# Rotating eight queries and both keys of a mixer at once, and normalising a unit's probabilities in one operation

## The chip, the cores and the metric

The kernel runs on one core of a Trainium2 chip. The metric is the time of one execution on the device in microseconds (us), lower is better; the kernel before has a median of 800.55 us over three runs (799.91 to 801.0). Five engines work side by side, each with its own queue in order: TensorE (PE in the profile; its weight loads are PEld), VectorE (DVE), ScalarE (ACT), GpSimd (POOL) and SyncE (SP), which here issues the DMAs. They wait for one another by semaphores.

## The reference

Two layers on 256 positions of width 1024, all in fp32. Each layer normalises its input (RMSNorm) and makes one projection `h @ w_in`, whose columns are divided among:

- mixer A: 8 queries, 2 keys and 2 values of 64 columns a head; attention in a window of 128 with a sink per head; queries and keys rotated by their position;
- mixer B: 8 queries; a compressed, a selected and a window branch, each with 2 keys and 2 values; the queries are used raw for the compressed branch and rotated for the two others, whose keys are rotated too. Three sigmoid gates a head weigh the branches;
- two merge gates of 1024 columns each.

The rotation is `concatenate([x1*cos - x2*sin, x2*cos + x1*sin])` on the two halves of a head. The probabilities of a head are `exp(s - m)` divided by their sum (for mixer A the sum and the sink's exponential). The outputs of the mixers are projected, gated, added, projected again and added to the input; then follows a gated feed-forward part with a short causal convolution (2816 inner columns), again with a norm on either side. With 256 positions the selected branch chooses all four blocks, so here it is plain causal attention, as the window branch is.

## The kernel before, in words

**Precision.** A factor of a matmul is split into a high and a low half (`copy` on ScalarE, L114, makes the high one; `sub` on VectorE, L117, the rest), and each product is three matmuls: high by high, high by low, low by high (`mm3`, L365). Weights come by DMA into `st`, four chunks deep, and are split into `wh` and `wl`.

**Tiling.** The 256 positions are two blocks t of 128. The input projection is cut into nine column tiles (IN_TILES); tile i takes four chunks of weights, and for each chunk and block six matmuls add into that block's bank. At its last chunk the tile's `fin` function reads the bank: `fin_a` (tile 0, eight queries of A), `fin_b` (tile 1), `fin_d` (tile 2: selected key and value, window key and value, 128 columns each, of mixer B), `fin_gate`, `fin_c` (tile 4). Banks of PSUM are taken by tag, two of each: "mm", "S", "T", "O". Tiles 2 and 3 both take "mm", so a block of tile 3 starts when the last reader of the like block of tile 2 is done.

**Rotation.** `rope` (L457) makes four VectorE instructions for h heads: `src * rs * cos` (L461), two halves of `src * rs * sin` (L463), and the sum (L465). `q_rot` (L477) does this for four queries, splits the result into a stacked tile `stk` of high and low halves and leaves `stack_T` for later, which transposes it with four matmuls (L472) and copies it into the query buffer. `k_rot` does the like for two keys of one branch. `v_split` writes the high half of two values with ScalarE and the low half with one VectorE instruction (L508) into VT, a zero-padded buffer; there is one VT for each of the three branches.

**Units.** A `Unit` is one block, one group of four heads and one or two branches. `scores` computes the scores in banks "S" (L588), a minimum per head on VectorE (L597) and the exponential on ScalarE (L600). `probs_T` makes one scale per head (L613 to L619), multiplies each head's probabilities by it with one VectorE instruction per head and branch (L622), transposes them (L628) and splits them. `values` multiplies by VT (L660 to L662). Each layer has four units of A (two of 4 heads x 128 columns, two of 4 x 256) and six of B: two with both branches (8 x 128) and four with one (4 x 256).

**Order.** Written work is put on a clock of parts: `part` advances it by one, `later(n, fn)` and `at(tick, fn)` put functions on later ticks, and PLAN and DL hold the ticks. The first tile of the first layer runs in the order as written on TensorE, VectorE and ScalarE (`manual_schedule`); everywhere else a planner orders each engine's instructions at build time, with modelled costs, by the order in which they were written among those that it holds ready. So a changed duration may change the order of other instructions. On the chip each engine keeps its order.

In the compressed branch of mixer B, `cmp_gelu` has ScalarE's tanh (L747) on the result of a chain of small GpSimd instructions (L730 to L741), and L748 on VectorE reads it.

## Time and profile before

| | |
|---|---|
| median of three runs | 800.55 us |
| the profiled execution | 800.75 us, of which the span from first to last instruction is 798.9 |
| mean granted TensorE clock | 0.991 |
| TensorE busy | 767.3 us (96%), 4745 matmuls |
| VectorE busy | 620.1 us (78%), 1280 instructions |
| ScalarE busy | 497.7 us (62%) |
| GpSimd busy | 44.2 us (6%) |

Busy time is the time in which at least one instruction of the engine runs; instructions of one engine overlap a little, so the next one may start before the one ahead of it ends. An instruction waits in its engine's queue until what it needs is there, and all behind it wait too. [...]

### The profile page before, as it was taken

The page shows a single profiled execution, that of the slowest core. Times are in us where ns is not written, and L with a number is a line of the kernel's source. Part 1 is how long each engine was busy: PE and PEld are TensorE (multiplying, and loading weights), DVE is VectorE, ACT ScalarE, POOL GpSimd, SP SyncE. Part 2 cuts the span into 40 slices and gives each one's busy share as a digit, 9 for nine tenths or more (in the row PEclk, how much of TensorE's full clock was granted, in tenths as well). Part 3 has the DMA queues.
Part 4 walks back from the last instruction along what each step waited for, and adds up shares of the span by engine and source line. Part 5 has one row for each costly group of instructions (what it writes and reads, how often), then busy time and mean ns, then how long its engine had stood idle before and what let it go on. Part 6 is the DMA issues. An engine that isn't in the chain of part 4 may idle for free.

```text
span 798.9 us, 13019 instructions
## 1 busy us (share of the span) xinstructions
PE 767.3 (96%) x4745; PEld 681.5 (85%) x4745; DVE 620.1 (78%) x1280; ACT 497.7 (62%) x952; POOL 44.2 (6%) x97
## 2 busy tenths in 40 slices
PE   7989989999899999999989999899998999999996
PEld 6778878888689999999968888888877999999995
DVE  5888888867768777777789999786867877767775
ACT  4678787755656555565555879667555655556552
POOL 2200022100200000000010000120001000000000
PEclk9998999999999999999999999999999999999998
DMA  7632156446556565665535232543545655656631
GB/s 266 226 100 89 61 155 202 133 162 182 191 177 186 185 185 186 207 216 185 182 106 179 90 119 78 196 162 132 187 156 170 199 185 185 185 185 210 213 106 53
DMA packets 42203, 131.26 MB, mean 164 GB/s; under 512 B 5359, under 2 KB 5915, under 8 KB 42139
## 3 DMA queue, kind: packets, MB, share of 16 engines
q1 hardware_dynamic: 41995, 130.18, 50.3%
q8 instruction: 37, 0.61, 0.3%
q10 hardware_dynamic: 144, 0.26, 0.1%
q14 instruction: 27, 0.22, 0.1%
HBM read 129.37 MB, written 1.05 MB: 163 GB/s over the span
## 4 chain that ended last, share of the span: by engine, by line
PE 81%; DVE 7%; ACT 6%; POOL 2%; issue 2%; DMA 1%; SPq 0%; DVEq 0%; POOLq 0%; ACTq 0%
PE mm L366 6%; PE mm L368 6%; PE mm L367 6%; PE S L367 5%; PE S L368 5%; PE S L366 5%; PE T L994 5%; PE T L993 5%; PE mm L994 5%; PE mm L993 5%; PE T L992 5%; PE mm L992 5%; PE O L366 3%; PE O L367 3%; PE O L368 3%; DVE wl L117 2%
## 5 line engine op out<-in xcount | busy, mean ns | idle before, releaser
L117 DVE TENSOR_TENSOR wl<-st,wh 128x1024 fp32r<-128x1024 f32 (+2 forms) x226 | 267.9, 1187 | 103.7 <-ACT wh L114 102.6
L114 ACT ACTIVATE wh<-st 128x1024 fp32r<-128x1024 f32 (+2 forms) x226 | 232.2, 1030 | 176.9 <-PE T L993 38.8
L366 PE MATMUL mm<-wh,x 128*128 128x512 f32 (+2 forms) x256 | 98.2, 384 | 3.4 <-DVE VT L508 2.4
L367 PE MATMUL mm<-wl,x 128*128 128x512 f32 (+2 forms) x256 | 95.8, 374 | 0.0
L368 PE MATMUL mm<-wh,x 128*128 128x512 f32 (+2 forms) x256 | 95.4, 373 | 0.1
L993 PE MATMUL mm<-q,wh 128*128 128x256 f32 x320 | 90.7, 283 | 0.0
L994 PE MATMUL T<-q,wl 128*128 128x256 f32 x320 | 90.6, 283 | 0.0
L993 PE MATMUL T<-q,wh 128*128 128x256 f32 x320 | 90.5, 283 | 0.0
L994 PE MATMUL mm<-q,wl 128*128 128x256 f32 x320 | 90.5, 283 | 0.0
L992 PE MATMUL T<-q,wh 128*128 128x256 f32 x320 | 90.5, 283 | 0.0
L992 PE MATMUL mm<-q,wh 128*128 128x256 f32 x320 | 90.5, 283 | 0.0
L992 PEld LDWEIGHTS mm<-q,wh 128*128 128x128 f32 x320 | 61.3, 192 | 0.9
L993 PEld LDWEIGHTS mm<-q,wh 128*128 128x128 f32 x320 | 61.3, 192 | 0.8
L992 PEld LDWEIGHTS T<-q,wh 128*128 128x128 f32 x320 | 61.3, 192 | 0.8
L993 PEld LDWEIGHTS T<-q,wh 128*128 128x128 f32 x320 | 61.3, 192 | 0.7
L994 PEld LDWEIGHTS mm<-q,wl 128*128 128x128 f32 x320 | 61.3, 192 | 0.1
L994 PEld LDWEIGHTS T<-q,wl 128*128 128x128 f32 x320 | 61.3, 192 | 0.0
L366 PEld LDWEIGHTS mm<-wh,x 128*128 128x128 f32 x256 | 49.5, 193 | 9.4 <-DVE VT L508 2.8
L368 PEld LDWEIGHTS mm<-wh,x 128*128 128x128 f32 x256 | 49.1, 192 | 6.6 <-DVE x L117 0.5
L367 PEld LDWEIGHTS mm<-wl,x 128*128 128x128 f32 x256 | 49.3, 193 | 5.2 <-DVE wl L117 0.4
L600 ACT ACTIVATE k<-k,mn 128x128 f32<-128x128 f32 (+1 forms) x96 | 42.6, 448 | 6.6 <-DVE mn L597 6.5
L114 ACT ACTIVATE k<-k 128x256 fp32r<-128x256 f32 x72 | 29.8, 414 | 10.8 <-DVE k L1005 5.8
(293 smaller groups left out, 1663.9 us busy)
## 6 DMA issues: line engine op xcount, KB each, us to landing
st<-in_ffn_w_up_dram SPq DMA_DIRECT2D x88, 512.0 KB, 4.2
st<-in_w_in_dram SPq DMA_DIRECT2D x48, 512.0 KB, 3.7
st<-in_ffn_w_down_dram SPq DMA_DIRECT2D x44, 512.0 KB, 3.7
st<-in_w_out_dram SPq DMA_DIRECT2D x16, 512.0 KB, 4.0
st<-in_w_in_dram SPq DMA_DIRECT2D x16, 384.0 KB, 3.2
st<-in_cmp_w_dram SPq DMA_DIRECT2D x16, 256.0 KB, 2.7
st<-in_w_branch_a_dram SPq DMA_DIRECT2D x8, 512.0 KB, 3.5
st<-in_w_branch_b_dram SPq DMA_DIRECT2D x8, 512.0 KB, 3.5
```

Of the source, the lines that this page charges most:

```text
L114: act.activation(dst, src, AF.Copy, scale=scale)
L117: dve.tensor_tensor(dst, a, b, ALU.subtract)
L366: pe.matmul(o, xh, wh, start=first, stop=False, skip_group_check=True)
L367: pe.matmul(o, xh, wl, start=False, stop=False, skip_group_check=True)
L368: pe.matmul(o, xl, wh, start=False, stop=last, skip_group_check=True)
L600: last_exp[0] = act.activation(self.pt[:, hh, s, :], sm[:, :nk], AF.Exp, bias=self.mn[:, i:i + 1], scale=-1.0, accum_out=self.dn[:, i:i + 1])
L992: pe.matmul(o, wh[:, k, :], hh[:, k, c0:c1], start=(k == 0), stop=False, skip_group_check=True)
L993: pe.matmul(o, wh[:, k, :], hl[:, k, c0:c1], start=False, stop=False, skip_group_check=True)
L994: pe.matmul(o, wl[:, k, :], hh[:, k, c0:c1], start=False, stop=(k == 7), skip_group_check=True)
```

## The change

`fin_a` rotates all eight queries of a block with one `rope` of eight heads, and then splits and stacks them in two parts of four. `fin_d` rotates the selected and the window keys with one `rope` of four heads. For that the columns of tile 2 are put in another order in the bank: the matmuls read the weights' pieces of 128 columns as key, key, value, value, where they lie as key, value, key, value. The four values of a block go with one ScalarE and one VectorE instruction into one buffer of 33 x 64 columns (VT33) in place of two; `values` takes its blocks from there by an offset. `probs_T` multiplies all probabilities of a unit by their scales, broadcast along the columns, in one instruction in place of four or eight. Mixer A's keys and values, and the queries of mixer B, go through the changed functions with the same instructions as before.

```diff
--- before.py
+++ after.py
@@ -316,7 +316,7 @@
         o = R_CB + l * 44 + jj
         return vec[:, o:o + 1]
 
-    VT = [cp.tile([P, 17 * 64], F32R, name=f"VT{i}") for i in range(3)]
+    VT = [cp.tile([P, n * 64], F32R, name=f"VT{n}") for n in (17, 33)]
     for v in VT:
         pool.memset(r32(v), 0.0)
 
@@ -436,7 +436,12 @@
                 tk = slice(t * P, (t + 1) * P)
                 for k in range(2):
                     kk = 2 * c + k
-                    mm3(bk[t][:, :w], xh[:, kk, tk], xl[:, kk, tk], ch[0][:, k, :], ch[1][:, k, :], kk == 0, kk == 7)
+                    o, wh, wl = bk[t][:, :w], ch[0][:, k, :], ch[1][:, k, :]
+                    if i == 2:
+
+                        o = o.rearrange("p (y x d) -> p y x d", x=2, y=2)
+                        wh, wl = [v.rearrange("p (x y d) -> p y x d", x=2, y=2) for v in (wh, wl)]
+                    mm3(o, xh[:, kk, tk], xl[:, kk, tk], wh, wl, kk == 0, kk == 7)
                 if c == 3:
                     fin(t, bk[t])
                 if tmajor and t == 1 and c < 2:
@@ -474,13 +479,16 @@
                 done.add(key)
             return fn
 
-        def q_rot(qT, t, h0, src, key, delay):
-            d = rope(src, t, True, 4)
-            stk = k2(F32R)
-            sv = stk.rearrange("p (h a d) -> p h a d", h=4, a=2)
-            copy(sv[:, :, 0, :], d)
-            sub(sv[:, :, 1, :], d, r32(sv[:, :, 0, :]))
-            later(delay, stack_T(stk, qT[:, h0:h0 + 4, t * P:(t + 1) * P], key, 0))
+        def q_rot(qT, t, h0, src, key, delays):
+            d = rope(src, t, True, 4 * len(delays))
+            for i, delay in enumerate(delays):
+                stk = k2(F32R)
+                sv = stk.rearrange("p (h a d) -> p h a d", h=4, a=2)
+                di = d[:, 4 * i:4 * i + 4, :]
+                copy(sv[:, :, 0, :], di)
+                sub(sv[:, :, 1, :], di, r32(sv[:, :, 0, :]))
+                h = h0 + 4 * i
+                later(delay, stack_T(stk, qT[:, h:h + 4, t * P:(t + 1) * P], (key[0], t, h // 4), 0))
 
         def q_raw(qT, t, h0, src, key, delay):
             if rq[t] is None:
@@ -492,27 +500,29 @@
             dve.scalar_tensor_tensor(sv[:, :, 1, :], src, rq[t], r32(sv[:, :, 0, :]), ALU.mult, ALU.subtract)
             later(delay, stack_T(stk, qT[:, h0:h0 + 4, t * P:(t + 1) * P], key, 0))
 
-        def k_rot(kT, t, src, key, delay):
-            rk = rope(src, t, False, 2)
-            stk = k2(F32R)
-            sv = stk.rearrange("p (g s a d) -> p g s a d", g=2, s=2, a=2)
-            kb = rk[:, :, None, :].to_broadcast([P, 2, 2, 64])
-            copy(sv[:, :, 0], kb)
-            sub(sv[:, :, 1], kb, r32(sv[:, :, 0]))
-            later(delay, stack_T(stk, kT[:, :, :, t * P:(t + 1) * P], key, 1))
-
-        def v_split(V, t, src, key):
+        def k_rot(t, src, dsts):
+            d = rope(src, t, False, 2 * len(dsts))
+            for i, (kT, key, delay) in enumerate(dsts):
+                stk = k2(F32R)
+                sv = stk.rearrange("p (g s a d) -> p g s a d", g=2, s=2, a=2)
+                kb = d[:, 2 * i:2 * i + 2, None, :].to_broadcast([P, 2, 2, 64])
+                copy(sv[:, :, 0], kb)
+                sub(sv[:, :, 1], kb, r32(sv[:, :, 0]))
+                later(delay, stack_T(stk, kT[:, :, :, t * P:(t + 1) * P], key, 1))
+
+        def v_split(V, n, t, src, keys):
             vb = V.rearrange("p (b d) -> p b d", d=64)
-            vh, vl = vb[:, t * 8 + 1:t * 8 + 6:4, :], vb[:, t * 8 + 3:t * 8 + 8:4, :]
+            o = t * 4 * n + 1
+            vh, vl = vb[:, o:o + 4 * n - 3:4, :], vb[:, o + 2:o + 4 * n - 1:4, :]
             copy(vh, src, scale=rs[t])
             dve.scalar_tensor_tensor(vl, src, rs[t], r32(vh), ALU.mult, ALU.subtract)
-            done.add(key)
+            done.update(keys)
 
         qA, qB, qR = big8("q8", 3), big8("q8", 3), big8("q8", 3)
         kA = ap_.tile([P, 2, 2, T], F32R, tag="kA", name=nm("kA"))
         kB = ap_.tile([P, 2, 2, 2, T], F32R, tag="kB", name=nm("kB"))
         kS, kW = kB[:, 0], kB[:, 1]
-        vA, vS, vW = VT
+        vA, vB = VT
         OB = [[None, None], [None, None]]
         OT = [None, None]
         GE = [None, None]
@@ -522,17 +532,16 @@
 
 
         def fin_a(t, b):
-            q_rot(qA, t, 0, heads(b, 0, 4), ("qA", t, 0), DL["qa0"])
-            q_rot(qA, t, 4, heads(b, 256, 4), ("qA", t, 1), DL["qa1"])
+            q_rot(qA, t, 0, heads(b, 0, 8), ("qA", t, 0), (DL["qa0"], DL["qa1"]))
 
         def fin_b(t, b):
-            k_rot(kA, t, heads(b, 0, 2), ("kA", t), DL["ka"])
-            v_split(vA, t, heads(b, 128, 2), ("vA", t))
-            q_rot(qB, t, 0, heads(b, 256, 4), ("qB", t, 0), DL["qb0"])
+            k_rot(t, heads(b, 0, 2), [(kA, ("kA", t), DL["ka"])])
+            v_split(vA, 2, t, heads(b, 128, 2), [("vA", t)])
+            q_rot(qB, t, 0, heads(b, 256, 4), ("qB", t, 0), (DL["qb0"],))
             q_raw(qR, t, 0, heads(b, 256, 4), ("qR", t, 0), DL["qr0"])
 
         def fin_c(t, b):
-            q_rot(qB, t, 4, heads(b, 0, 4), ("qB", t, 1), DL["qb1"])
+            q_rot(qB, t, 4, heads(b, 0, 4), ("qB", t, 1), (DL["qb1"],))
             q_raw(qR, t, 4, heads(b, 0, 4), ("qR", t, 1), DL["qr1"])
             for kd in range(2):
                 kvd[t][kd] = k2()
@@ -544,10 +553,8 @@
                 later(DL["cb1"], lambda: cmp_blocks(1))
 
         def fin_d(t, b):
-            k_rot(kS, t, heads(b, 0, 2), ("kS", t), DL["ks"])
-            v_split(vS, t, heads(b, 128, 2), ("vS", t))
-            k_rot(kW, t, heads(b, 256, 2), ("kW", t), DL["kw"])
-            v_split(vW, t, heads(b, 384, 2), ("vW", t))
+            k_rot(t, heads(b, 0, 4), [(kS, ("kS", t), DL["ks"]), (kW, ("kW", t), DL["kw"])])
+            v_split(vB, 4, t, heads(b, 256, 4), [("vS", t), ("vW", t)])
 
         def fin_gate(i):
             c0, w = IN_TILES[i]
@@ -617,9 +624,8 @@
                     e = self.co[:, 0:4]
                     dve.tensor_tensor(e, e, self.dn, ALU.add)
                 dve.reciprocal(e, e)
-                for i in range(n):
-                    p = self.pt[:, i // ns, i % ns, :]
-                    dve.tensor_scalar(p, p, e[:, i:i + 1], None, ALU.mult)
+                p = self.pt.rearrange("p h s c -> p (h s) c")
+                dve.tensor_tensor(p, p, e[:, :, None].to_broadcast([P, n, self.nk]), ALU.mult)
                 self.ph = []
                 for s in range(ns):
                     for kb in range(t + 1):
@@ -643,8 +649,8 @@
                         c = slice(par * 256, par * 256 + 256)
                         v = []
                         for part_ in range(2):
-                            blk = 1 + 2 * ((kb * 2 + g) * 2 + part_) - par
-                            v.append(V[:, blk * 64:blk * 64 + P])
+                            blk = 1 + 2 * ((kb * V[2] + V[1] * 2 + g) * 2 + part_) - par
+                            v.append(V[0][:, blk * 64:blk * 64 + P])
                         mm3_(ov, v, ph[:, c], pl[:, c], first)
                         first = False
                 done.add(("O", self.br, t, g, self.sets[0][3]))
@@ -830,7 +836,7 @@
 
 
         B = lambda k: base + k
-        sA, sS, sW = (kA, vA, "kA", 0), (kS, vS, "kS", 1), (kW, vW, "kW", 2)
+        sA, sS, sW = (kA, (vA, 0, 2), "kA", 0), (kS, (vB, 0, 4), "kS", 1), (kW, (vB, 1, 4), "kW", 2)
         for (t, g), tick in zip(((0, 0), (0, 1), (1, 0), (1, 1)), PLAN["A"]):
             e = Unit(t, g, 0, qA, "qA", [sA], m_band).plan(B(tick))
             if t == 1:
```

## Rows read from the trace of the kernel before

**Rows 1.** The page: busy us (share) by engine; chain of waits by engine.

```profile
PE 767.3 (96%) x4745; PEld 681.5 (85%) x4745; DVE 620.1 (78%) x1280; ACT 497.7 (62%) x952; POOL 44.2 (6%) x97
...
PE 81%; DVE 7%; ACT 6%; POOL 2%; issue 2%; DMA 1%; SPq 0%; DVEq 0%; POOLq 0%; ACTq 0%
```

**Rows 2.** TensorE's waits: who <- for whom: us in total, times, longest us.

```profile
PE T L628 <- DVE k L622: 3.9, 3, 2.0
...
PE mm L366 <- DVE VT L508: 2.4, 2, 1.8
```

**Rows 3.** Timeline, TensorE, 53 to 58.4: start, us, what, [idle before <-releaser].

```profile
53.71 0.96 PE L588 MATMUL S<-kA,q 128*128 128x128 f32 x7
55.36 0.28 PE L472 MATMUL T<-ident_r,k 128*128 128x128 f32 x1 [0.69 <-ACT k L114]
...
58.36 0.60 PE L366 MATMUL mm<-wh,x 128*128 128x280 f32 x1 [1.79 <-DVE VT L508]
```

**Rows 4.** Windows: stretch, us, busy (x) of PE, PEld, DVE, ACT, POOL, clock, DMA.

```profile
57.40:64.20 6.80, 5.84 (x25) 5.83 (x26) 5.01 (x23) 3.87 (x14) 0.00 (x0) 0.50 0.00 0
65.50:75.00 9.50, 7.89 (x60) 7.41 (x60) 9.27 (x34) 9.50 (x32) 0.00 (x0) 1.00 0.31 104
455.00:465.00 10.00, 10.00 (x81) 9.62 (x80) 9.91 (x33) 10.00 (x31) 0.00 (x0) 1.00 0.30 93
507.95:511.30 3.35, 3.35 (x16) 3.28 (x16) 2.60 (x12) 2.35 (x7) 0.00 (x0) 0.50 0.02 6
```

**Rows 5.** Timeline of VectorE, then of ScalarE, 53 to 58 us.

```profile
53.14 0.34 DVE L461 SCALAR_TENSOR_TENSOR k<-mm,rstd,tab 128x128 f32<-128x128 f32 x1
...
57.96 0.35 DVE L508 SCALAR_TENSOR_TENSOR VT<-mm,rstd,VT 128x128 fp32r<-128x128 f32 x1
...
54.16 0.36 ACT L114 ACTIVATE VT<-mm,rstd 128x128 fp32r<-128x128 f32 x1
...
56.92 0.36 ACT L114 ACTIVATE VT<-mm,rstd 128x128 fp32r<-128x128 f32 x1
```

**Rows 6.** Timeline of VectorE, 67 to 75 us.

```profile
67.60 0.87 DVE L622 TENSOR_SCALAR k<-k,co 128x128 f32<-128x128 f32 x4
...
71.28 1.22 DVE L117 TENSOR_TENSOR wl<-st,wh 128x1024 fp32r<-128x1024 f32 x1
72.41 0.68 DVE L117 TENSOR_TENSOR k<-T,k 128x512 fp32r<-128x512 f32 x1
73.01 1.13 DVE L622 TENSOR_SCALAR k<-k,co 128x256 f32<-128x256 f32 x4
```

**Rows 7.** Groups by line and shape: count | busy us, mean ns | idle.

```profile
L461 DVE SCALAR_TENSOR_TENSOR k<-mm,rstd,tab 128x256 f32<-128x256 f32 x12 | 5.7, 479 | 1.8 <-POOL tab L348 1.8
```

**Rows 8.** Timeline of VectorE in both layers, around 94, 444 and 481 us.

```profile
94.53 0.20 DVE L619 RECIPROCAL co<-co 128x8 f32<-128x8 f32 x1
...
444.38 0.34 DVE L461 SCALAR_TENSOR_TENSOR k<-mm,rstd,tab 128x128 f32<-128x128 f32 x1
...
481.60 0.20 DVE L619 RECIPROCAL co<-co 128x8 f32<-128x8 f32 x1
```

**Rows 9.** Timeline of VectorE, then of TensorE, 27 to 29 us.

```profile
27.10 1.22 DVE L117 TENSOR_TENSOR wl<-st,wh 128x1024 fp32r<-128x1024 f32 x1
...
28.37 0.50 PE L367 MATMUL S<-wl,x 128*128 128x512 f32 x1 [1.16 <-DVE wl L117]
```

**Rows 10.** Timeline of VectorE, then of TensorE, 119 to 121 us.

```profile
119.44 0.19 DVE L748 SCALAR_TENSOR_TENSOR z<-z,z 128x32 f32<-128x32 f32 x1 [1.63 <-ACT z L747]
119.55 1.13 DVE L622 TENSOR_SCALAR k<-k,co 128x256 f32<-128x256 f32 x4
...
120.05 0.41 PE L628 MATMUL T<-cst,k 128*128 128x128 f32 x2 [1.74 <-DVE k L622]
```

**Rows 11.** Timeline of TensorE: scores on kB in two pieces, then in one.

```profile
87.40 1.11 PE L588 MATMUL S<-kB,q 128*128 128x256 f32 x8
...
130.15 0.64 PE L588 MATMUL S<-kB,q 128*128 128x256 f32 x4
```

## The prediction

> **What bounds the kernel now.** I read the page's first part, then the waits of TensorE, then its timeline where the waits are long, then VectorE and ScalarE in the same stretch. TensorE is busy 767.3 of 798.9 us [rows 1], so only its 31.6 us of idle time, and what it loses where it is busy at half clock, can be won; VectorE (78%) and ScalarE (62%) matter only where TensorE waits for them, and VectorE is 7% of the chain of waits [rows 1]. The waits say which of its idle time ends on an instruction of this change: 3.9 us in three waits for the normalised probabilities (L622) and 2.4 us in two waits for the low half of the second mixer's values (L508) [rows 2]. Everything else that TensorE waits for is left as it is.
>
> The place that matters most is in layer 0, after the input tile of the second mixer's keys and values. That tile and the next one share two "mm" banks, so the next tile can't start before the last reader of a bank is done, and for block 0 that is L508 for the window values. TensorE finishes its scores at 54.67 (53.71 + 0.96), waits 0.69 us, does a few short instructions and waits 1.79 us more until 58.36 [rows 3]. The granted clock is 0.50 (1.2 of 2.4 GHz) from 57.40 to 64.20, right behind this idle time, and TensorE is busy for 5.84 us of it [rows 4]: at full clock that is half, so 2.9 us are lost on top of the 2.5 us of waits. A second half-clock stretch of 3.35 us stands behind the longest L622 wait in layer 1 [rows 4].
>
> **The bank release in layer 0 (fin_d).** Now: VectorE starts on block 0 at 53.14 and the last read ends at 58.31 (57.96 + 0.35), 5.17 us later [rows 5]. The work itself is small; it is strung out because the second v_split comes last: ScalarE makes the first split's high half at 54.16 and the second's only at 56.92, because instructions for other work were put between. The fused version needs one ScalarE copy of 128x256, which can stand where the first stands now, and one VectorE split behind it. How long: an instruction's own cost is its step to the next start, some 0.09 us less than its duration (the 1024-wide subtraction lasts 1.22 us and the next one starts 1.13 us later [rows 6]). Scalar-tensor-tensor on PSUM lasts 0.34 us for 128 [rows 5] and 0.479 us for 256 elements [rows 7], some 1.07 ns an element; so steps of 0.26 and 0.39 us, 0.19 for 64 and 0.67 for 512. Plain tensor-tensor has steps of 1.13 us for 1024 and 0.60 for 512 elements [rows 6], which by the same line makes 0.33 for 256 and 0.20 for 128.
> - Two key rotations now: 2 x (0.26 + 2 x 0.19 + 0.20) = 1.68 us. One of four heads: 0.39 + 2 x 0.26 + 0.33 = 1.24. Saved 0.44, four times: 1.8 us.
> - Two low halves now 2 x 0.26 = 0.52; one of 256: 0.39. Saved 0.13, four times: 0.5 us. ScalarE saves about as much.
> The new release of block 0's bank is then 53.14 + 1.24 + 0.39 = 54.77, and with an allowance of 0.4 for a hand-over and an instruction of other work in between about 55.2 instead of 58.31. TensorE is free at 54.67 and its 2.5 us of waits shrink to about 0.6. With that little idle time I expect no half-clock stretch. Gross gain: 1.9 + 2.9 = 4.8 us. How much survives is best read from layer 1, which runs the same code without the half clock: from the first key rotation to the reciprocal of the second mixer's first unit it takes 481.60 - 444.38 = 37.22 us, in layer 0 94.53 - 53.14 = 41.39 us [rows 5, 8]. So layer 0 can win 4.2 us before it runs like layer 1. I take 4.0. Bounds: 0 (the new order puts the copy late again) and 5.4 us (all waits and the whole half-clock loss). In layer 1 the release is hidden better; I take 0.3 us for it, between 0 and 1.
>
> **The rotation of eight queries (fin_a).** Now per block 2 x (0.39 + 2 x 0.26 + 0.33) = 2.48 us of VectorE; fused 0.67 + 2 x 0.39 + 0.60 = 2.05. Saved 0.43, four times 1.7 us. But the three long instructions come before the weight split on which TensorE waits 1.16 us at 28.37 [rows 9]: 0.67 + 2 x 0.39 = 1.45 us ahead of it where 0.39 + 2 x 0.26 = 0.91 stand now. If the split stays behind them, TensorE waits 0.5 us longer, once, in layer 0. I take +0.5 (bounds 0 and +1, the latter if the later first stack adds a wait of the same size). Layer 1's fin_a has slack and counts nothing.
>
> **The normalisation.** tensor_scalar steps are (0.87 - 0.09)/4 = 0.195 us for 128 and (1.13 - 0.09)/4 = 0.26 us for 256 elements, one tensor_tensor 0.60 us for 512 and 1.13 us for 1024 [rows 6]; the broadcast scale is taken as free, as I see nothing against it. A unit of four heads of 128 goes from 0.78 to 0.60 (four of them), one of eight of 128 from 1.56 to 1.13 (four), one of four of 256 from 1.04 to 1.13 (twelve): -0.7 - 1.7 + 1.1 = -1.3 us of VectorE in the whole kernel. So this edit is not the saving that the durations suggest, since the removed instructions overlap.
>
> [...]
>
> What the edit moves is the first transposition. Now TensorE's first transposition may start after the first head, as at 120.05, 0.50 us after the first tensor_scalar at 119.55 [rows 10]; with one instruction it has to wait for all heads, 1.22 us plus the same 0.15 us hand-over, so 0.87 us later. At 15 of 20 units TensorE now starts within that reach of the first tensor_scalar. The order of TensorE is planned with the instructions' costs, so the planner should put 0.87 us of input-projection matmuls ahead of the transpositions, and these then run without pacing. The long waits at 120.05 and 507.41 aren't made by the normalisation at all: VectorE stands 1.63 us at L748, which waits for ScalarE's tanh behind GpSimd's chain, and L622 is queued behind it [rows 10]. Those stay. I take +0.3 us net, bounds -1.5 (the two waits that VectorE's interruptions of the eight-head units cause go, and some of the others) and +9.5 (next part).
>
> **The permuted reading** of the weights in pieces of 128 columns: the scores that read keys in two pieces of 128 take (1.11 - 0.28)/7 = 0.12 us each, those that read 256 in a row (0.64 - 0.28)/3 = 0.12 [rows 11]. Nothing.
>
> **Sum.** The profiled execution took 800.75 us (1.85 around its span of 798.9), 0.2 above the median of the runs, 800.55. -4.0 - 0.3 + 0.5 + 0.3 = -3.5, so 797.25 for such an execution and 797.05 against the median; forecast 797.1.
>
> **Rivals.**
> - The gain is given back at once by ScalarE and VectorE. Right after the stretch, from 65.50 to 75.00, ScalarE is busy 9.50 of 9.50 us and VectorE 9.27, with TensorE idle for 1.61 [rows 4]: if their exponentials, not TensorE, set the pace there, TensorE only arrives earlier and waits longer. Of 4 us some 0.5 stay: 800. Against it: in layer 1 the like stretch has ScalarE at 10.00 of 10 and TensorE at 10.00 as well [rows 4].
> - The other side: the planner finds nothing to put ahead of the transpositions, or keeps their place. Then each of the 15 units adds what the later start exceeds its present slack: 0.87 at 120.05 [rows 10], between 0.2 and 0.94 at the others, 9.5 us in sum over the trace's starts. The other three terms gain 3.8 us: 800.75 + 9.5 - 3.8 = 806.5, and with half of it 801.7. It decides from 3.8 us on, which is about six of the 15 starts not filled; from there on the kernel isn't faster.
> - The change does what it says but the permuted reading costs: 96 matmuls read that way; at the rate of half a clock each would need 0.21 us more, 20 us in all: 817. The rows above speak against it.
>
> **Chances.** The forecast's case 0.60, with 793.5 to 798.9 as its own range. Gain given back 0.17. Transpositions late 0.20, mostly at 801 to 804. Permuted reading 0.03. About 0.2% (1.6 us) can be told from no change. Faster: 0.60 and a little of the second case, 0.62; same 0.17; slower 0.21. Range 793.5 to 802.5, which leaves the far part of the third case and the last one out.
>
> **What will show it.** Right: the L508 wait of TensorE gone or under 0.6 us at the place of 58.36, no half clock behind it, the distance of 41.39 us near 37 to 38. The L622 waits at the places of 120.05 and 507.41 still there with VectorE standing at L748. Wrong: a half-clock stretch still there; more transposition waits than three with a sum over 6 us; a longer step of the matmuls of the key and value tile; the weight split of rows 9 more than 1 us later than now.

## The result, and the profile after

The changed kernel takes 794.61 us (median of four runs, 794.26 to 795.35), the kernel before 800.61 beside it: ratio 0.9927, 95% interval 0.9910 to 0.9944. Its profiled execution took 794.85 us (span 793.0, mean granted clock 0.992), 5.9 less than the 800.75 of before. The forecast was 797.1 within 793.5 to 802.5. In the changed kernel the line numbers lie 5 to 8 higher: L508 is now L518, L622 is L628, L628 is L634, L748 is L754.

The page (busy us and share by engine; the chain of waits by engine), for [rows 1]. The number of VectorE's instructions and its busy time fell, 620.1 to 613.2 us; TensorE's share of the chain did not change, and its idle time went from 31.6 to 27.3 us (793.0 - 765.7); 1.4 of these 4.3 us are a shorter wait for the first DMA (2.8 and 1.4 us), ahead of the first projection matmul, which starts at 11.16 us in both kernels, so they aren't part of the gain:

```profile
PE 765.7 (97%) x4745; PEld 682.0 (86%) x4745; DVE 613.2 (77%) x1168; ACT 495.4 (62%) x948; POOL 48.1 (6%) x96
...
PE 81%; DVE 7%; ACT 7%; POOL 2%; issue 2%; DMA 1%; SPq 0%; DVEq 0%; POOLq 0%; ACTq 0%
```

TensorE's waits (who <- for whom: us in total, times, longest us), for [rows 2]. Both groups of before are gone from the list (normalised probabilities, 3.9 us; VT, 2.4 us). Two others of 3.3 and 2.4 us are new, and the one for the weight split is longer:

```profile
PE S L718 <- DVE mn L604: 3.3, 2, 1.7
...
PE T L477 <- ACT q L114: 2.4, 2, 1.3
PE S L367 <- DVE wl L117: 1.9, 2, 1.4
```

So 5.7 of those 6.3 us came back at other instructions: what is gained is not the sum of the waits that went. The windows (stretch, us, busy (x) of PE, PEld, DVE, ACT, POOL, clock, DMA), for [rows 4], show what did not come back in layer 0 and what is new: 3.41 us of half clock where 6.80 stood, TensorE without a pause from 65.5 to 75, no half clock at 508, but two new half-clock stretches, at 401.56 (the border of the layers) and 445.94 (layer 1's key and value tile). Between the start and the end of the kernel both profiled executions have 10.2 us of half clock, 6.83 + 3.41 before and three times 3.41 after, at other places:

```profile
56.80:60.21 3.41, 3.41 (x18) 3.40 (x18) 3.10 (x17) 3.41 (x15) 0.00 (x0) 0.51 0.00 0
65.50:75.00 9.50, 9.50 (x69) 8.80 (x68) 8.45 (x20) 9.14 (x25) 0.00 (x0) 1.00 0.59 182
401.56:404.97 3.41, 3.41 (x11) 2.84 (x11) 2.87 (x5) 1.21 (x3) 1.64 (x5) 0.51 0.46 150
445.94:449.35 3.41, 3.41 (x18) 3.39 (x17) 3.41 (x18) 3.41 (x15) 0.00 (x0) 0.51 0.00 0
...
507.95:511.30 3.35, 3.35 (x27) 3.24 (x25) 3.19 (x5) 1.95 (x4) 0.00 (x0) 1.00 0.90 306
```

The place of `fin_d` in layer 0: TensorE's timeline (start, us, what, [idle before <-releaser]), for [rows 3]. The next tile's first matmul (L366, 280 columns) starts at 54.72 with no wait, where it started at 58.36. Then a new wait of 1.08 us for ScalarE's copy of `q`:

```profile
52.96 1.00 PE L595 MATMUL S<-kA,q 128*128 128x128 f32 x8
...
54.72 0.29 PE L366 MATMUL mm<-wh,x 128*128 128x280 f32 x1
...
56.34 0.53 PE L477 MATMUL T<-ident_r,k 128*128 128x128 f32 x4 [1.08 <-ACT q L114]
```

VectorE, then ScalarE, in the same stretch, for [rows 5]. From the first rotation at 50.41 to the end of block 0's last read (52.11 + 0.49) are 2.2 us, where 5.17 were. That first rotation also starts 2.73 us earlier (53.14 before). ScalarE's one VT copy stands right in front of that read. Its q copies (55.72) stand behind a table load and four exponentials, hence the new wait:

```profile
50.41 0.48 DVE L466 SCALAR_TENSOR_TENSOR k<-mm,rstd,tab 128x256 f32<-128x256 f32 x1
...
52.11 0.49 DVE L518 SCALAR_TENSOR_TENSOR VT<-mm,rstd,VT 128x256 fp32r<-128x256 f32 x1
...
51.49 0.47 ACT L114 ACTIVATE VT<-mm,rstd 128x256 fp32r<-128x256 f32 x1 [1.03 <-DVE k L468]
...
52.77 1.28 ACT L607 ACT_TABLE_LOAD   x1
...
55.72 1.05 ACT L114 ACTIVATE q<-T 128x512 fp32r<-128x512 f32 x2
```

VectorE, then TensorE, at the weight split behind `fin_a`, for [rows 9]: the split starts 0.51 us later, TensorE waits 1.44 us instead of 1.16.

```profile
27.61 1.22 DVE L117 TENSOR_TENSOR wl<-st,wh 128x1024 fp32r<-128x1024 f32 x1
...
28.88 0.50 PE L367 MATMUL S<-wl,x 128*128 128x512 f32 x1 [1.44 <-DVE wl L117]
```

The compressed branch in layer 0, for [rows 10]: VectorE, then ScalarE, then TensorE. The unit is normalised (109.87) before VectorE comes to the gelu product (L754), no longer behind it. ScalarE's tanh still stands 3.21 us for GpSimd, and TensorE now waits 1.68 us for `mn`, the minima that VectorE takes of the next unit's scores:

```profile
109.87 1.23 DVE L628 TENSOR_TENSOR k<-k,co 128x1024 f32<-128x1024 f32 x1
...
113.42 0.19 DVE L754 SCALAR_TENSOR_TENSOR z<-z,z 128x32 f32<-128x32 f32 x1 [1.38 <-ACT z L753]
...
113.16 0.23 ACT L753 ACTIVATE z<-z 128x32 f32<-128x32 f32 x1 [3.21 <-POOL z L747]
...
116.17 0.67 PE L718 MATMUL S<-wj,M 128*80 128x256 f32 x4 [1.68 <-DVE mn L604]
```

The n-th projection matmul of one timeline is set beside the n-th of the other. The differences of their starts give the balance (us, after minus before, summed up from the start):

| place | change there | balance |
|---|---|---|
| `fin_a` and what follows, layer 0 | +0.1 | +0.1 |
| keys and values of the second mixer, layer 0 | -5.8 | -5.7 |
| compressed branch, layer 0 | -0.5 | -6.2 |
| border of the layers | +1.2 | -5.0 |
| keys and values, layer 1 | +1.7 | -3.3 |
| compressed branch, layer 1 | -2.6 | -5.9 |

### The profile page after: what moved, and what is told of

It is laid out like the page before. It is cut to its first block, busy times and chain, and to the rows that moved or that the text cites. A ratio compares the mean times of both kernels' runs of the same rounds, so it can differ in the third digit from the quotient of the medians.

```text
span 793.0 us, 12908 instructions
## 1 busy us (share of the span) xinstructions
PE 765.7 (97%) x4745; PEld 682.0 (86%) x4745; DVE 613.2 (77%) x1168; ACT 495.4 (62%) x948; POOL 48.1 (6%) x96
## 4 chain that ended last, share of the span: by engine, by line
PE 81%; DVE 7%; ACT 7%; POOL 2%; issue 2%; DMA 1%; SPq 0%; DVEq 0%; POOLq 0%; ACTq 0%
PE mm L366 6%; PE mm L367 6%; PE mm L368 6%; PE S L367 5%; PE S L368 5%; PE S L366 5%; PE T L1000 5%; PE T L999 5%; PE mm L1000 5%; PE mm L999 5%; PE T L998 5%; PE mm L998 5%; PE O L366 3%; PE O L367 3%; PE O L368 3%; DVE wl L117 2%
## 5 line engine op out<-in xcount | busy, mean ns | idle before, releaser
L117 DVE TENSOR_TENSOR wl<-st,wh 128x1024 fp32r<-128x1024 f32 (+2 forms) x226 | 268.0, 1188 | 101.1 <-ACT wh L114 99.7
L366 PE MATMUL mm<-wh,x 128*128 128x512 f32 (+2 forms) x256 | 97.3, 382 | 0.1
L366 PEld LDWEIGHTS mm<-wh,x 128*128 128x128 f32 x256 | 49.2, 193 | 5.8 <-ACT k L114 0.4
L354 POOL TENSOR_SCALAR rstd<-s 128x1 f32<-128x1 f32 x16 | 6.1, 381 | 520.7 <-ACT k L362 520.5
```

The costliest lines, as they stand in the source:

```text
L117: dve.tensor_tensor(dst, a, b, ALU.subtract)
L354: pool.tensor_scalar(r, s2[:, 0:1], s2[:, 1:2], EPS, ALU.add, ALU.add)
L366: pe.matmul(o, xh, wh, start=first, stop=False, skip_group_check=True)
```

## The experiments

Each median stands beside the kernel before on the same chip (800.37 to 801.13 us). Single executions of one kernel differ by 4 to 5 us: the kernel before took 797.76 to 802.30 us in 23 executions on one chip, with mean granted clocks of 0.989 to 0.997, the longer ones at the lower clocks. One stretch of 3.41 us at half clock takes 0.002 off that mean (an estimate: half of 3.41 in 799 us), so the same kernel has up to some four such stretches more or less. So a half-clock stretch seen in a single profile can't be credited to an edit without other traces. TensorE's wait for the first DMA differs too, 1.4 to 3.8 us in the profiles.

| edit | us | ratio, 95% interval |
|---|---|---|
| `fin_a` alone | 794.87 | 0.9926 (0.9909 to 0.9943) |
| `fin_d` alone | 811.97 | 1.0139 (1.0120 to 1.0158) |
| normalisation alone | 799.02 | 0.9974 (0.9961 to 0.9987) |
| `fin_a` and normalisation | 795.72 | 0.9938 (0.9914 to 0.9962) |
| `fin_a` and `fin_d` | 804.20 | 1.0039 (1.0024 to 1.0054) |
| `fin_d` and normalisation | 795.52 | 0.9941 (0.9923 to 0.9960) |
| all three (the change) | 794.61 | 0.9927 (0.9910 to 0.9944) |

The change's four executions had mean clocks of 0.992 and 0.993, the 23 of the kernel before a median of 0.992: the 6 us are not a matter of the clock. `fin_a` alone had a median of 0.9955. A rough estimate of a time without half clock, the time multiplied by the clock, is 794.3 us before, 790.5 for `fin_a` alone and 788.6 for the change; so the two other edits may give some 2 us that half clock takes back, which the times by themselves don't show.

**`fin_d` alone,** with the functions and the permuted reading that it needs.

```diff
-            k_rot(kS, t, heads(b, 0, 2), ("kS", t), DL["ks"])
-            v_split(vS, t, heads(b, 128, 2), ("vS", t))
-            k_rot(kW, t, heads(b, 256, 2), ("kW", t), DL["kw"])
-            v_split(vW, t, heads(b, 384, 2), ("vW", t))
+            k_rot(t, heads(b, 0, 4), [(kS, ("kS", t), DL["ks"]), (kW, ("kW", t), DL["kw"])])
+            v_split(vB, 4, t, heads(b, 256, 4), [("vS", t), ("vW", t)])
```

> The kernel before with the changed fin_d alone (both keys rotated at once, one split of four values, the permuted reading). If the early release of block 0's bank makes the gain: 3 to 5 us faster than before (795.5 to 797.5), the wait of 1.79 us and the half-clock stretch behind it in layer 0 gone, and the new wait on a query copy of 1.1 to 1.4 us there as in the changed kernel. If the normalisation makes the gain: within 1 us of before.

Slower, by 11.3 us: neither of the two expected times. In layer 0's key and value tile it gains as foreseen: like matmuls are 1.5 us late at 47 us (a half-clock stretch at the start, which six of the fourteen profiled executions have) and 4.1 early at 78. VectorE begins there when it did before, if those 1.5 us are taken off, and is done after 2.51 us instead of 5.17; the wait for VT is gone:

```profile
54.66 0.47 DVE L466 SCALAR_TENSOR_TENSOR k<-mm,rstd,tab 128x256 f32<-128x256 f32 x1
...
56.69 0.48 DVE L518 SCALAR_TENSOR_TENSOR VT<-mm,rstd,VT 128x256 fp32r<-128x256 f32 x1 [0.16 <-ACT VT L114]
```

So the release works as predicted where it was predicted. The expected wait for a query's copy is 0.17 us there; one of 1.33 us stands in layer 1 instead. And the matmuls are 1.6 us late behind layer 0's compressed branch, 3.3 late behind layer 1's key and value tile, and 11.2 late at 546 us. About half of that is half clock: three stretches in layer 1, 13.7 us long together, where before had one of 3.41. The longest group in the list of TensorE's waits, with 2.95 us in front of the late place in layer 0 and 3.15 in layer 1:

```profile
PE T L636 <- DVE k L630: 10.6, 6, 3.2
```

These are the transpositions behind the normalisation, which this kernel still does head by head. So the part that carried the forecast makes the kernel slower by itself.

**Normalisation alone.**

```diff
-                for i in range(n):
-                    p = self.pt[:, i // ns, i % ns, :]
-                    dve.tensor_scalar(p, p, e[:, i:i + 1], None, ALU.mult)
+                p = self.pt.rearrange("p h s c -> p (h s) c")
+                dve.tensor_tensor(p, p, e[:, :, None].to_broadcast([P, n, self.nk]), ALU.mult)
```

> The kernel before with the one-operation normalisation alone. If it is worth next to nothing, as the steps say (1.3 us of VectorE, mostly hidden): 799 to 801.5. If the 2.6 us that layer 1 gains behind its key tile come from it: 797 to 798.5, with the L622 waits of 1.74 and 2.03 us gone or shifted. If the later start of the transpositions costs: over 802.

1.7 us faster, 799.02, within the first of the three expected ranges. The VT wait of 1.79 us stays and so does the half clock behind it. The waits of [rows 10] turn into waits of 1.70 and 1.60 us for `mn`, at nearly the same places, and the half clock at 508 is gone.

**`fin_a` alone,** with `q_rot` as in the change.

```diff
-            q_rot(qA, t, 0, heads(b, 0, 4), ("qA", t, 0), DL["qa0"])
-            q_rot(qA, t, 4, heads(b, 256, 4), ("qA", t, 1), DL["qa1"])
+            q_rot(qA, t, 0, heads(b, 0, 8), ("qA", t, 0), (DL["qa0"], DL["qa1"]))
```

> The kernel before with the rotation of eight queries alone. My step: 0 to +1 us (800.6 to 801.6), the wait on the weight split at 28.4 us in layer 0 longer by 0.3 to 0.6 us. Rival: the 0.43 us of VectorE saved four times come through, 1 to 1.7 us faster.

5.9 us faster, as much as the whole change, by a part to which I had given +0.5; both expectations fell. The gain is at a place that the edit doesn't touch. VectorE, then ScalarE, then TensorE at `fin_d`, whose code is that of before:

```profile
51.13 0.34 DVE L461 SCALAR_TENSOR_TENSOR k<-mm,rstd,tab 128x128 f32<-128x128 f32 x1
...
54.12 0.35 DVE L511 SCALAR_TENSOR_TENSOR VT<-mm,rstd,VT 128x128 fp32r<-128x128 f32 x1
...
53.72 0.37 ACT L114 ACTIVATE VT<-mm,rstd 128x128 fp32r<-128x128 f32 x1
...
56.25 0.29 PE L366 MATMUL mm<-wh,x 128*128 128x280 f32 x1
```

VectorE comes to the first rotation 2.0 us earlier than before (51.13, 53.14), and the last read ends 3.3 us after it (before: 5.17) with the same small steps: ScalarE's second copy follows 1.8 us behind its first one, not 2.8. There is no wait for VT and no half clock here. So this stall needed no shorter `fin_d`; another order was enough, as a shorter `fin_d` was enough in the kernel above.

**Values first:** before, with both splits written ahead of both key rotations.

```diff
+            v_split(vS, t, heads(b, 128, 2), ("vS", t))
+            v_split(vW, t, heads(b, 384, 2), ("vW", t))
             k_rot(kS, t, heads(b, 0, 2), ("kS", t), DL["ks"])
-            v_split(vS, t, heads(b, 128, 2), ("vS", t))
             k_rot(kW, t, heads(b, 256, 2), ("kW", t), DL["kw"])
-            v_split(vW, t, heads(b, 384, 2), ("vW", t))
```

> The kernel before, nothing fused: in fin_d the two v_splits are only written ahead of the two k_rots. If what counts is when the last reader of the bank is done, not how many instructions there are: 2.5 to 5 us faster (795.5 to 798), the wait on L508 of 1.79 us gone. If the saved VectorE time is what counts: within 1 us of before.

800.49 us, ratio 1.0003 (0.9989 to 1.0017). The wait for VT is gone and the kernel is 8.2 us ahead at 65 us; 4.7 at 78; 2.3 behind the border of the layers, where this trace has 6.83 us of half clock; 0 in layer 1. Of each of these leads 1.3 us come from a shorter wait for the first DMA. This is like the first rival of the prediction, only later: a stall removed early was given back in full at other places. The half clock can't be the whole of it, since the twelve executions had a median clock of 0.996, more than the 0.992 of the kernel before. So removing this stall is not enough for a gain; the order of all that follows counts as well.

**`fin_a` and normalisation:** both diffs above on the kernel before.

> The rotation of eight queries and the one-operation normalisation, without the changed fin_d. Theory now: each edit acts by the order that the planner makes, and the stall behind the key tile of layer 0 goes with fin_a's edit alone (5.9 us faster by itself), so fin_d's edit isn't needed: 792.5 to 795, and layer 1's key tile without the wait of 1.34 us and the half clock that the changed kernel has there. Rival: fin_d's shorter work is what makes the changed kernel fast, and this one is 2 us or more slower than it, 796.5 to 799.

795.72 us, between the two expected ranges. Layer 1's key tile is free of the wait of 1.34 us and of the half clock, as the theory says. The interval overlaps that of `fin_a` alone: a gain by the normalisation is not shown here.

**`fin_a` and `fin_d`, and `fin_d` and normalisation.**

> Two of the three parts: eight queries rotated at once in the first mixer, both keys rotated and the values split at once in the second; the normalisation stays in its several operations. Theory (the 11 us that the second part costs alone come from the order in which it places the unit's work behind the gelu product, and another order is free of them): 794 to 799, with no TensorE wait over 2.5 us in the compress regions. Rival (the second part makes that stand whatever stands beside it, and only the one-operation normalisation takes it away): 804 to 808, with the waits of about 3 us at the tile k near 140 and 535 us.

> Two of the three parts: both keys rotated and the values split at once in the second mixer, and the normalisation in one operation; the first mixer's queries as before. Theory (order): 795 to 800, no wait of about 3 us on the tile k in the compress regions. If the second part makes the stand whatever stands beside it: about 810, the loss of the second part alone (11.3 us) less the 1.6 us that the normalisation gave alone. If this one is at 795 to 800 and the other pair at 804 to 808, the normalisation is what takes the loss away; if both are under 800, any change of order does.

804.20 and 795.52 us. With `fin_d`, normalising head by head costs 9 us (1.0039 against 0.9927) to 16 us (1.0139 against 0.9941); without `fin_d` 2 us (0.9974) or nothing that shows. So the one operation is what takes `fin_d`'s loss away. Beside it `fin_d` gains 2.6 us without `fin_a` (0.9941 against 0.9974), and nothing that shows with it (0.9927 against 0.9938). VectorE's timeline of layer 1's second half shows where; first `fin_a` and `fin_d`, with TensorE's wait in the last line:

```profile
522.51 0.16 DVE L620 TENSOR_SCALAR co<-dn 128x4 f32<-128x4 f32 x1
525.37 0.19 DVE L755 SCALAR_TENSOR_TENSOR z<-z,z 128x32 f32<-128x32 f32 x1 [2.69 <-ACT z L754]
...
527.87 1.14 DVE L629 TENSOR_SCALAR k<-k,co 128x256 f32<-128x256 f32 x4
...
528.37 0.41 PE L635 MATMUL T<-cst,k 128*128 128x128 f32 x2 [3.15 <-DVE k L629]
```

and `fin_d` with the normalisation:

```profile
519.28 1.23 DVE L629 TENSOR_TENSOR k<-k,co 128x1024 f32<-128x1024 f32 x1
522.74 0.19 DVE L755 SCALAR_TENSOR_TENSOR z<-z,z 128x32 f32<-128x32 f32 x1 [2.24 <-ACT z L754]
```

VectorE stands 2.2 to 2.7 us at the gelu product in both; only in the first are the normalising operations queued behind it, and TensorE behind them. `fin_a` with `fin_d` lost less than `fin_d` alone: 7.3 us in such waits, not 10.6, and none near 140 us. The theory that any change of order would be free of the loss fell: `fin_a` changes the order too, and 7.3 us of these waits stay.

**Queries earlier.** The two new waits for q in layers 0 and 1 suggest an earlier transposition of them: the changed kernel with `qb0` and `qr0` one tick sooner.

```diff
-DL = {..., 'qb0': 8, 'qr0': 8, ...}
+DL = {..., 'qb0': 7, 'qr0': 7, ...}
```

> The changed kernel with the stacks of mixer B's first four queries (qb0, qr0) one tick earlier, so that ScalarE's query copies stand ahead of its table load and the first exponentials. If the new waits of 1.08 and 1.34 us and the half clock behind them come from those copies standing behind the exponentials: both gone, 2.5 to 4.5 us faster than the changed kernel, 790 to 792. If VectorE or the banks hold TensorE there anyway: within 1 us of it, 793.6 to 795.6.

794.44 us, ratio 0.9924 (0.9903 to 0.9944): the same as the change. Both waits are gone, and in this trace all half clock between the start and the end, but 4.3 us of other waits came in, and the gain that was expected of it did not come. Window and waits:

```profile
56.80:60.21 3.41, 2.56 (x22) 2.33 (x21) 3.07 (x14) 3.41 (x17) 0.00 (x0) 1.00 0.00 0
...
PE T L477 <- ACT k L114: 2.8, 4, 0.9
...
PE S L595 <- ACT k L114: 1.5, 1, 1.5
```

**The same edit on the kernel before.**

> The kernel before with the same stacks one tick earlier, nothing else. If the wait of 1.79 us and the half clock in layer 0 are an accident of the planned order: gone without any of the three edits, 795 to 797.5. If the second v_split's place makes them: still there, within 1 us of before, 799.6 to 801.6.

799.43 us, ratio 0.9987 (0.9973 to 1.0000). The VT wait shrinks from 1.79 to 1.14 us and the half clock behind it from 6.83 to 3.41; 2.9 us are gained there, 1.3 are left behind the border of the layers, where a half-clock stretch appears (405.5). The median is just outside both expected ranges, and whether anything remains is not settled.

**Gelu later.** My theory was that the waits for `mn` come from VectorE's stand at the gelu product, so that writing `cmp_gelu` five ticks later would remove them.

```diff
-DL = {..., 'ge': 3, ...}
+DL = {..., 'ge': 8, ...}
```

> The changed kernel with cmp_gelu eight ticks behind its transposition in place of three, which moves the waiting VectorE instruction (the product behind the tanh) some 15 places back in VectorE's order. If VectorE's standing at it is what makes TensorE wait 1.68 and 1.60 us: both gone, 2.5 to 4 us faster than the changed kernel, 790.5 to 792. If TensorE waits there for its scores anyway: within 1 us of it.

797.67 us, ratio 0.9962 (0.9948 to 0.9976): slower than the change. The theory fell. VectorE no longer stands at the gelu product in the first half of the compressed branch, and TensorE still waits 1.4 us there, once in each layer, with another wait of 1.7 us behind each. ScalarE's timeline shows what is left, with TensorE's waits above it:

```profile
PE T L634 <- DVE kc L775: 3.4, 2, 1.7
...
PE S L718 <- DVE mn L604: 2.8, 2, 1.4
...
113.22 0.23 ACT L753 ACTIVATE z<-z 128x32 f32<-128x32 f32 x1 [3.01 <-POOL z L747]
```

ScalarE itself stands 3 us at the tanh, and the copies queued behind it are late for whoever waits for them. VectorE's stand followed from ScalarE's; the next two runs test this.

**Gelu on VectorE.** The nine small operations before the tanh on VectorE in place of GpSimd, in the changed kernel and in `fin_a` alone. (The second text calls the `fin_a` edit by another name; the edit is the rotation of eight queries.)

```diff
-            pool.tensor_tensor(bs, hs[:, 2:3], hs[:, 12:13], ALU.add)
+            dve.tensor_tensor(bs, hs[:, 2:3], hs[:, 12:13], ALU.add)
...
-            pool.tensor_tensor(z3, z3, z, ALU.mult)
+            dve.tensor_tensor(z3, z3, z, ALU.mult)
```

> The changed kernel with the nine small GpSimd operations between a unit's hidden sums and the tanh of its gelu put on VectorE. Theory (the TensorE waits of 1.68 and 1.60 us on mn at L718 begin with ScalarE's tanh, which stands 3.21 us for GpSimd's z): ScalarE's stand and both waits fall below 0.5 us, VectorE's stand at the gelu product goes, and the time falls by 2 to 4 us against the changed kernel, to 790.5 to 792.5. Rival (the wait is made by how much VectorE and ScalarE have to do there, and nine more operations on VectorE only move it): other waits of 1 to 2 us on VectorE's or ScalarE's tiles in the same stretches, and a time within 1 us of the changed kernel, 793.6 to 795.6.

> The kernel before with the one-query-copy part of the change (the weight split with both halves in one step, eight queries rotated at once) and the nine small GpSimd operations of the gelu on VectorE. Theory: its waits of 1.95 us at 114.00 and 1.69 us at 501.08 fall below 0.5 us, so 791 to 792.5 against 794.87 without the move. Rival: they are replaced by waits on VectorE of the same length, 794 to 796.

792.64 us, ratio 0.9899 (0.9881 to 0.9917), and 790.98 us, ratio 0.9882 (0.9863 to 0.9901), the fastest of all: 2.0 us under the change and 3.9 under `fin_a` alone. The step from `fin_a` alone is beyond the intervals (0.9882 against 0.9926); the one from the change isn't quite, they overlap by a little (0.9917 against 0.9910), and 792.64 is 0.1 above the expected range. But the waits for `mn` and VectorE's stands are gone from its trace as the theory says; ScalarE's stand falls to 0.71 us, not below 0.5. The two fastest kernels' intervals overlap, so with this mended no gain by `fin_d` and the one operation is shown. ScalarE, changed kernel with the gelu on VectorE:

```profile
111.90 0.58 ACT L114 ACTIVATE k<-T 128x512 fp32r<-128x512 f32 x1
113.19 0.23 ACT L753 ACTIVATE z<-z 128x32 f32<-128x32 f32 x1 [0.71 <-DVE z L747]
```

The tanh is not earlier: 113.19 against 113.16. Nor is the chain ahead of it shorter: from its first operation to its last it takes 4.67 us on GpSimd (108.46 to 113.13) and 5.70 on VectorE (107.46 to 113.16), where other work stands in between. What changed is the tanh's place. With GpSimd's chain ScalarE takes it behind the unit's exponentials and one weight split (109.13, 0.83 us) and stands. Now two more weight splits and two copies stand ahead of it, and it stands 0.71 us. The planner places by modelled times; the order would fit a model that takes the GpSimd chain for some 3 us too short, but the model itself was not measured. The move changes the engine and the order together, so that it acts by the place is read from these two timelines and not tested apart.

## Why the prediction was right, and where it wasn't

The time fell within the range, 2.5 us below the forecast, but its account of where the time goes holds for one place only, the bank release in layer 0; that the sum came so near is luck. The part that was to carry the gain makes the kernel slower by itself, and the part that was to cost gives as much by itself as the whole change.

**The bank release in layer 0 (-4.0): the place and the sign right, the size short, the cause too narrow.** The wait of 1.79 us is gone, TensorE has no idle time at 54.72, and the distance of 41.39 us is 38.55 (50.41 to 88.96, where the reciprocal starts), just outside the 37 to 38 that were named. The stretch gained 5.8 us. Release in 2.2 us where 1.63 + 0.4 were expected: that step held, and `fin_d` alone shows it too (2.51 us). Four things did not hold. The sum let VectorE begin at 53.14 as before; it begins at 50.41, and of the 5.71 us by which the last read ends earlier (58.31, now 52.60) 2.73 come from that. `fin_a` alone begins earlier as well (51.13), `fin_d` alone doesn't. "With that little idle time I expect no half-clock stretch": one of 3.41 us follows the new wait for q. The bound of 5.4 us was exceeded, since layer 0 kept gaining further on, where TensorE had been idle for 1.61 us (65.50 to 75.00) and no longer is. And the shorter work was enough but not needed: `fin_a` alone and the values put first remove the same stall. Besides, the 2.9 us lost at half clock were counted as for half the speed; in the kernel before, matmuls of 280 columns follow one another after 0.234 us there (58.76 to 60.40) and after 0.13 at clock 1.00 (69.16 to 69.68), which makes 2.6 of the 5.84 us (an estimate from these steps).

**The bank release in layer 1 (-0.3): wrong, +1.7.** What failed is the step that looked only at the release. The new wait there and the half clock behind it cost more than the release gave:

```profile
445.18 0.54 PE L477 MATMUL T<-ident_r,k 128*128 128x128 f32 x4 [1.34 <-ACT q L114]
```

This wait, of 1.33 to 1.35 us, stands in all six traces that have the changed `fin_d` with the queries' stacks on their old tick, with half clock behind it in all six, and in none of the eight others. So here it is `fin_d` that makes it.

**`fin_a` (+0.5): the direct cost right, the effect wrong.** The split starts 0.51 us later as computed, and TensorE's wait is 0.28 us longer; by 44 us the two kernels are level again (0.07 us). That the edit reorders what comes behind it, and is alone worth 5.9 us, was not in the sum. "Layer 1's fin_a has slack and counts nothing" looked at the wrong effect in the same way.

**The normalisation (+0.3): durations right, effect wrong in sign and size.** One operation of 1024 elements takes 1.143 us to the next start and one of 512 takes 0.610 (1.13 and 0.60 foreseen). The weight split of 1024 elements (L117), which has no broadcast operand, takes 1.142 in median in the same trace, so the broadcast scale costs nothing that shows. But alone the normalisation gains 1.7 us, in the trace 0.3 in layer 0's compressed branch and 1.3 in layer 1's; in the whole change these branches gained 3.1 us. "The planner should put 0.87 us of input-projection matmuls ahead" held in so far as no wait for the normalised probabilities is left in the list. The sentence "Those stay" on the waits at 120.05 and 507.41 failed: VectorE stood at the gelu product ahead of the normalisation, and the new order has the normalisation first. The waits became waits of 1.68 and 1.60 us for `mn`. The half clock at 508 went too, but `fin_a` alone, which keeps its waits for the probabilities (3.8 us), has none there either. Without this edit the other two would be a loss of 3 us.

**The border of the layers (+1.2): not in the prediction at all.** Nothing of the change lies there. Both kernels wait 1.58 and 1.27 us for the same tile; only the changed one then has half clock in its profile. The last section shows that this half clock comes and goes among kernels that don't differ there, so the runs don't show these 1.2 us to be the change's doing.

**The rivals.** "Gain given back" did not happen to the whole change but is what "values first" did. "Transpositions late" was the wrong way round: the transpositions that were late were those behind the separate operations. Times on the slower side, which was priced at 801.7 to 806.5 us, were measured (804.2 and 812.0), but in the two versions with `fin_d` and without the one operation, so not by the mechanism of that rival. The permuted reading costs nothing that shows: the matmuls of that tile follow one another after 0.23 us in both kernels (52.05 to 52.28 in the changed one, 51.76 to 51.99 before), where the same size takes 0.43 at half clock (402.63 to 403.06).

The forecast of 797.1 missed 2.5 us of gain, and that is what is left of larger errors, by place: 3.4 too little gain in the compressed branches, 1.8 in layer 0 and 0.4 for `fin_a`, against 2.0 too much in layer 1's key tile and 1.2 at the border.

What stays open is why the planner, given `fin_a`'s eight-query rotation near 27 us, orders VectorE's and ScalarE's work at `fin_d`, some 25 us further on, in the better way. The runs show that it does, not which of its choices turned.

## What to carry to other kernels

Where a planner orders the work, an edit has two effects, its own cost and a new order, and here the second was the larger one: parts that gave -5.9, +11.3 and -1.7 us alone gave -6.0 together. Predict the first from durations, put a range of several us on the second, and time each part alone before crediting it. When an engine waits, follow the chain to the instruction that stands first: TensorE waited for VectorE, VectorE for ScalarE, and what had to be mended was ScalarE's place for one tanh behind a chain on GpSimd.

## What the runs showed of the hardware

**The same wait may cost half clock or not.** TensorE waits 1.58 and 1.27 us at the border of the layers in both kernels. Its timeline after:

```profile
399.49 0.66 PE L373 MATMUL T<-cst,k 128*128 128x128 f32 x4 [1.58 <-DVE k L405]
401.42 0.99 PE L373 MATMUL T<-cst,k 128*128 128x128 f32 x4 [1.27 <-DVE k L405]
```

followed by the window of 401.56 shown above, at clock 0.51, in which matmuls of 512 columns follow one another after 0.43 us (402.63 to 404.76, five steps); before, the same two waits are followed by clock 1.00, and the step is 0.23 us (409.20 to 410.80, seven steps):

```profile
405.73 0.66 PE L373 MATMUL T<-cst,k 128*128 128x128 f32 x4 [1.58 <-DVE k L405]
407.66 0.66 PE L373 MATMUL T<-cst,k 128*128 128x128 f32 x4 [1.27 <-DVE k L405]
...
405.50:409.50 4.00, 2.42 (x13) 1.66 (x14) 3.82 (x7) 3.06 (x10) 1.76 (x5) 1.00 0.12 30
```

The wait for q in layer 0 does the like: 1.08 us in the change, then half clock; 1.09 us with the gelu on VectorE, and the window behind it is at full clock:

```profile
56.24 0.54 PE L477 MATMUL T<-ident_r,k 128*128 128x128 f32 x4 [1.09 <-ACT q L114]
...
56.30:60.21 3.91, 3.91 (x33) 3.89 (x34) 3.40 (x20) 3.91 (x17) 0.00 (x0) 1.00 0.00 0
```

The two waits at the border stand in all fourteen traces, within 0.02 us of the same length, and half clock follows them in nine, of 3.41 or 6.83 us, and not in five. In the change the border's stretch cost 1.2 us. So at these places the length of the wait doesn't tell whether it costs clock as well, though at others half clock follows each time (the wait for q in layer 1, six of six).

At half clock 512 columns in 0.426 us are 1.2 columns a ns; at full clock 512 columns take 0.107 us more than 256, 2.4 columns a ns (before, steps of 0.227 from 559.71 to 566.28 and of 0.120 from 704.09 to 706.13). The profile gives the clock as a share alone, so the 1.2 of 2.4 GHz beside it in the prediction stand for these rates.

**One small GpSimd operation has two durations.** In the changed kernel the addition of L743 (32 elements) takes 0.27 us in the second half of the compressed branch and 1.07 in the first, in both layers; the scalar addition of L742, the other way round, 1.31 and 0.41. The nine operations together take 4.7 us in all four places. The profile's spans on GpSimd are rough, and what makes the long ones is not shown. On VectorE L743 takes 0.21 (the changed kernel with the gelu on VectorE), so GpSimd takes 1.3 to 5 times as long for it. Both lines in layer 1 (duration in ns min/median/max, first and last start):

```profile
L742 POOL TENSOR_SCALAR z<-hs,bs x2: 410/864/1319, 498.7 to 519.3; 128x32 f32<-128x32 f32 x2
```

```profile
L743 POOL TENSOR_TENSOR z<-z,hs x2: 266/670/1073, 499.2 to 520.7; 128x32 f32<-128x32 f32 x2
```
